# GpSimd in place of VectorE for the fifteen elimination steps of each recurrent chain

## The chip, the core and the metric

The kernel runs on one core of one Trainium2 chip. The metric is the device time of one execution in microseconds; the time before is the median of 3 runs. A profile is one execution taken by the hardware profiler. Its engines are PE (TensorE; PEld is its weight load), DVE (VectorE), ACT (ScalarE), POOL (GpSimd) and SP (SyncE, which here only issues DMAs). Each engine works through its own instructions in the order in which they were built, and an instruction waits on semaphores for what it needs from the others.

## The reference, cut to what matters

A decoder trunk of two layers over 512 tokens of width 1024. Each layer is a half-step SwiGLU feed-forward, a token mixing, and another feed-forward. The mixing runs three kinds of heads side by side on one projection: sliding-window attention, RWKV-7 time mixing (4 heads of 64) and a short convolution.

```python
for l in range(DEPTH):
    h = h + 0.5 * (1.0 + gt1) * swiglu(hn, w_ffn1_in[l], w_ffn1_out[l])
    proj = hn @ w_mix_in[l]
    y_att = sliding_window_sink_attention(p_att, ...)
    y_rwkv = rwkv7_time_mix(p_rwkv, ...)
    y_conv = short_conv_mix(p_conv, conv_w[l])
    h = h + (1.0 + gt2) * (jnp.concatenate([y_att, y_rwkv, y_conv], axis=-1) @ w_mix_out[l])
    h = h + 0.5 * (1.0 + gt3) * swiglu(hn, w_ffn2_in[l], w_ffn2_out[l])

def step(S, inp):        # in rwkv7_time_mix, scanned over the tokens
    s_kk = jnp.einsum('bhvk,bhk->bhv', S, kk_t)
    S = S * w_t[:, :, None, :] - s_kk[..., None] * (kk_t * a_t)[:, :, None, :] + v_t[..., None] * k_t[:, :, None, :]
    return S, jnp.einsum('bhvk,bhk->bhv', S, r_t)
```

## The kernel before, in words

The activations lie transposed, with features on the 128 partitions and the 512 tokens along the free dimension. Weights come from DRAM in tiles of 128x1024, and each is split into a high and a low part (L101 on ACT, L102 on DVE), so that a product is three matmuls (L90 to L92, L98).

The mixing (`mix`, from L585) weaves four generators: `products` makes the projections and, later, the output products; `rwkv(0)` and `rwkv(1)` are the recurrent chains, each with two of the four heads (called chain 0 and chain 1 here); `attention` is the attention. A loop at its end takes steps of the chains and the attention and puts projection matmuls between them in proportion to their estimated work. Then the scheduler of the tile framework sets the final order of each engine's instructions from the dependencies and its own model of durations; only passages under `manual_schedule` keep their written order. So a line that goes to another engine can change the order on all of them.

A recurrent chain does not scan over 512 tokens. It works in 8 chunks of 64, and inside a chunk the recurrence is a triangular system whose inverse is needed. The way to that inverse, in program order:

- DVE prepares the decayed operands: the running decay P (L783), its reciprocal iP (L791), the reciprocal of a norm rn (L792), kk (L794), the bonus (L800, which the head sum ps_bo of PE reads), AR, be and ka (L805 to L812).
- PE multiplies them (`pairs`, L824) into ps_c, and DVE masks the result into B (L828), whose first half LT holds the strictly triangular systems; K follows in the same way.
- The 64 diagonal blocks of 16x16 (2 heads, 8 chunks, 4 blocks) are gathered one to a partition: LT is written to DRAM as dl (L836), and eight DMAs read it back as G (L846), 64 partitions of 256 columns.
- GpSimd fills V_ (the tile `inv`) with unit matrices (L848, L849).
- Fifteen steps of elimination invert the 64 blocks side by side, each with a multiply into `elim` (L853) and a subtract in `inv` (L854): 30 instructions, each of which needs the one before it. They are 15 to 64 columns wide on 64 partitions, 680 columns in the fifteen multiplies and as many in the subtracts.
- `inv` goes to DRAM as di (L856) and comes back as C (L859, eight DMAs), from which DVE makes T (L907) and its transpose TT (L908).
- Two levels of products (L916 on PE into ps_x, ps_t and ps_tt; L921, L925, L928 on DVE) raise the inverse from blocks of 16 to 64. Then follow ps_w (L935), the chunk transitions ps_gn and ps_o (L946 to L969), and six short state steps ps_s (L977, L978).

There are two such chains in each of two layers, four in all, and 120 of the elimination instructions. The DMAs of dl, G, di and C stand in SP's queue among the loads of weights (`load_w`, L267). GpSimd's queue holds, in the feed-forwards, loads of conditioning weights (L177) and accumulating loads (L395), and in the mixing only fills.

Of the kernel before, what the change touches and what calls it, by code (L numbers as in the profile page):

```python
# [12 lines left out]
ALU = mybir.AluOpType  # L13
# [44 lines left out]
def trunk_kernel(ctx, tc, ins, out, layers=L, phases=("ffn1", "mix", "ffn2")):  # L58
    nc = tc.nc
# [11 lines left out]
    tt, stt, ts = nc.vector.tensor_tensor, nc.vector.scalar_tensor_tensor, nc.vector.tensor_scalar  # L71
# [46 lines left out]
    for i in range(KD):  # L118
        t = hp_.tile([P, T], F32, name=f"h{i}")
# [15 lines left out]
    for name, v in (("eps", EPS), ("eps64", 64 * EPS), ("gneps", GN_EPS), ("nhb", -HB)):  # L135
        t = const.tile([P, 1], F32, name=f"v_{name}")
# [71 lines left out]
    def square(i, sl):  # L208
        sq = E("sq")[:, sl]
        act(sq, h[i][:, sl], AF.Square)  # L210
        return sq
# [373 lines left out]
    def mix(l, hn, ss, mp, then, ready):  # L585
# [14 lines left out]
        def EQ(q, name):  # L600
            return mp.tile([P, T], F32, name=name, tag=f"e{q}", bufs=2)
# [154 lines left out]
        def rwkv(q):  # L756
# [38 lines left out]
            t = EQ(q, "k2")  # L795
# [42 lines left out]
            NT = 2 * NM * 2 * NB  # L838
            square = lambda t: t[:NT, : BASE * BASE].rearrange("p (t u) -> p t u", u=BASE)
            G = square(EQ(q, "G"))  # L840
            for c in range(2):
                for m in range(NM):
                    n = (c * NM + m) * 2 * NB
# [3 lines left out]
            V_ = square(EQ(q, "inv"))  # L847
            nc.gpsimd.memset(V_, 0.0)  # L848
            nc.gpsimd.memset(V_.rearrange("p t u -> p (t u)")[:, :: BASE + 1], 1.0)  # L849
            for s in range(BASE - 1):  # L850
                n = BASE - 1 - s
                t = mp.tile([NT, BASE * BASE // 4], F32, name="elim", tag=f"el{q}")[:, : n * (s + 1)].rearrange("p (t u) -> p t u", u=s + 1)
                tt(t, G[:, s, s + 1 :].unsqueeze(2).to_broadcast([NT, n, s + 1]), V_[:, s : s + 1, : s + 1].to_broadcast([NT, n, s + 1]), ALU.mult)  # L853
                tt(V_[:, s + 1 :, : s + 1], V_[:, s + 1 :, : s + 1], t, ALU.subtract)  # L854
            di = dram.tile([2 * NM, 2 * NB, BASE, BASE], F32, name="di", tag=f"di{q}", bufs=2)
            nc.sync.dma_start(di.rearrange("m n t u -> (m n) t u"), V_)  # L856
            C_ = EQ(q, "C")[:, : 2 * NB * BASE].rearrange("p (n u) -> p n u", u=BASE)
# [223 lines left out]

        prod = products()
        live, waiting = {}, {"rwkv0": lambda: rwkv(0), "rwkv1": lambda: rwkv(1), "att": attention}
        left, fill, credit = 2 * RWKV_WORK + ATT_WORK, FILL_WORK, 0.0
        more = True
# [286 lines left out]
```

## Time and profile before

| what | value |
|---|---|
| median of 3 runs | 1912.6 us (1911.94 to 1915.08) |
| profiled execution, its own time | 1913.21 us |
| its span, first to last instruction | 1911.2 us |
| granted TensorE clock, mean | 0.996 |
| mixing of the first layer | about 400 to 620 us of the span |
| mixing of the second layer | about 1340 to 1560 us of the span |
| DMA, mean | 161 GB/s |

A row of a group reads: line, engine, operation, tile written <- tiles read, shapes, count; then busy us, mean ns of one; then the idle time of the engine ahead of them and what ended it. A row of a timeline begins with the start in us from the span's start and the duration in us; a bracket gives the idle time before it and what ended that. The view by stretches gives the busy us of each engine in a stretch of the span. Tiles have the kernel's names; in rows of the built order a number behind a name tells copies of a tile apart.

### The profile page before, as it was taken

The numbers are of one execution on the slowest core, as the hardware profiler recorded it, in microseconds if no ns is written. First come the engines' busy times: TensorE is split into PE (matmuls) and PEld (weight loads), VectorE is DVE, ScalarE is ACT, GpSimd is POOL, SyncE is SP. The second block draws the span as 40 slices with busy tenths as digits, with TensorE's granted clock in tenths as the row PEclk, the third lists the DMA queues.
The fourth block names the chain that finished last, engine by engine and source line by source line (L and its number), as shares of the span: only waits on it lengthen the run. The fifth ranks groups of instructions, "written<-read, shape, count | busy, mean of one in ns | idle before, by whom it ended". The sixth has DMA issues, their size and how long they took to land. (4 is left out here: it accounts for less than half of the span.)

```text
span 1911.2 us, 37042 instructions
## 1 busy us (share of the span) xinstructions
PE 1878.8 (98%) x15504; PEld 1741.7 (91%) x15504; DVE 1399.8 (73%) x2181; ACT 837.0 (44%) x1264; POOL 130.7 (7%) x212
## 2 busy tenths in 40 slices
PE   8999999999999999999999999999999999999999
PEld 7998899897888999899899989989878899988998
DVE  7687687758976877677877776876599667864862
ACT  4443255346322554155345514544562235532551
POOL 0101100100000001110100020010000000110000
PEclk8999999999999999999999999999999999999999
DMA  7767877521312476887727678781321315774741
GB/s 300 245 168 221 271 198 229 168 70 45 79 43 81 123 198 176 278 218 199 264 62 193 171 260 242 191 278 42 93 61 49 88 34 163 209 217 130 198 140 59
DMA packets 104326, 308.46 MB, mean 161 GB/s; under 512 B 23392, under 2 KB 24416, under 8 KB 103136
## 3 DMA queue, kind: packets, MB, share of 16 engines
q1 hardware_dynamic: 75936, 203.33, 32.9%
q0 software_dynamic: 28224, 102.77, 21.7%
q8 instruction: 121, 1.98, 0.4%
q14 instruction: 45, 0.37, 0.1%
HBM read 302.66 MB, written 3.41 MB: 160 GB/s over the span
## 5 line engine op out<-in xcount | busy, mean ns | idle before, releaser
L101 ACT CAST wH<-wraw 128x1024 fp32r<-128x1024 f32 (+2 forms) x292 | 268.4, 922 | 512.6 <-PE ps_mm L91 176.8
L102 DVE TENSOR_TENSOR wL<-wraw,wH 128x1024 fp32r<-128x1024 f32 (+2 forms) x292 | 308.1, 1058 | 96.9 <-ACT wH L101 95.8
L90 PE MATMUL ps_mm<-actH,wH 128*128 128x512 f32 (+1 forms) x784 | 288.5, 368 | 0.0
L91 PE MATMUL ps_mm<-actL,wH 128*128 128x512 f32 (+1 forms) x784 | 288.0, 367 | 0.0
L92 PE MATMUL ps_mm<-actH,wL 128*128 128x512 f32 (+1 forms) x784 | 288.0, 367 | 0.0
L441 PE MATMUL ps_d<-comH,wH 128*128 128x256 f32 x816 | 226.8, 278 | 1.6 <-ACT wH L101 0.8
L443 PE MATMUL ps_d<-comH,wL 128*128 128x256 f32 x816 | 225.8, 277 | 2.3 <-DVE wL L102 2.3
L442 PE MATMUL ps_d<-comL,wH 128*128 128x256 f32 x816 | 225.5, 276 | 0.0
L98 PE MATMUL ps_mm<-hnH,wH 128*128 128x256 f32 x1040 | 214.0, 286 | 5.1 <-ACT hnH L101 2.9
L98 PE MATMUL ps_mm<-hnL,wH 128*128 128x256 f32 x1040 | 211.8, 283 | 0.0
L98 PE MATMUL ps_mm<-hnH,wL 128*128 128x256 f32 x1040 | 209.5, 281 | 0.5 <-DVE wL L102 0.5
L163 DVE SCALAR_TENSOR_TENSOR wada<-wada,crep 128x1024 f32<-128x1024 f32 x140 | 168.0, 1220 | 47.8 <-DMA wada<-in_wadaT 47.6
L102 DVE TENSOR_TENSOR wL<-sum,wH 128x1024 fp32r<-128x1024 f32 x102 | 124.8, 1224 | 74.9 <-ACT wH L101 74.7
L98 PEld LDWEIGHTS ps_mm<-hnH,wH 128*128 128x128 f32 x1040 | 159.5, 190 | 16.1 <-issue 8.2
L92 PEld LDWEIGHTS ps_mm<-actH,wL 128*128 128x128 f32 x784 | 147.8, 189 | 24.4
L90 PEld LDWEIGHTS ps_mm<-actH,wH 128*128 128x128 f32 x784 | 147.8, 189 | 24.2
L91 PEld LDWEIGHTS ps_mm<-actL,wH 128*128 128x128 f32 x784 | 147.8, 189 | 24.1
L101 ACT CAST wH<-sum 128x1024 fp32r<-128x1024 f32 x102 | 107.5, 1054 | 140.3 <-PE ps_d L442 60.1
L98 PEld LDWEIGHTS ps_mm<-hnL,wH 128*128 128x128 f32 x1040 | 160.2, 190 | 6.7 <-issue 5.7
L98 PEld LDWEIGHTS ps_mm<-hnH,wL 128*128 128x128 f32 x1040 | 160.1, 190 | 4.1 <-issue 2.9
L441 PEld LDWEIGHTS ps_d<-comH,wH 128*128 128x128 f32 x816 | 153.2, 188 | 3.9 <-ACT wH L101 1.4
L443 PEld LDWEIGHTS ps_d<-comH,wL 128*128 128x128 f32 x816 | 153.2, 188 | 2.9 <-DVE wL L102 2.9
(402 smaller groups left out, 4237.3 us busy)
## 6 DMA issues: line engine op xcount, KB each, us to landing
wada<-in_wadaT POOLq DMA_DIRECT2D x128, 512.0 KB, 4.9
wraw<-in_wmi SPq DMA_DIRECT2D x40, 512.0 KB
wraw<-in_w2p SPq DMA_DIRECT2D x36, 512.0 KB
wraw<-in_w1p SPq DMA_DIRECT2D x32, 512.0 KB
wraw<-in_w1o SPq DMA_DIRECT2D x32, 384.0 KB
wraw<-in_w2o SPq DMA_DIRECT2D x32, 384.0 KB
wraw<-in_w1i SPq DMA_DIRECT2D x20, 512.0 KB
wraw<-in_w1o SPq DMA_DIRECT2D x32, 320.0 KB
```

Of the source, the lines that this page charges most:

```text
L90: mm(acc, wH, xH, start=start, stop=False)
L91: mm(acc, wH, xL, start=False, stop=False)
L92: mm(acc, wL, xH, start=False, stop=stop)
L98: mm(acc[:, sl], w[a][:, k], x[b][:, sl], start=start and n == 0 and sl is HALVES[0], stop=stop and n == 2, skip_group_check=True)
L101: nc.scalar.copy(hi, src)
L102: nc.vector.tensor_sub(lo, src, hi.bitcast(F32))
L163: stt(w, w, 1.0, crep, ALU.mult, ALU.mult, accum_out=out_)
L441: mm(pt[:, i], wH, x[k][0], start=start and i + k == 0, stop=False, skip_group_check=True)
L442: mm(pt[:, i], wH, x[k][1], start=False, stop=False, skip_group_check=True)
L443: last = mm(pt[:, i], wL, x[k][0], start=False, stop=k == 3, skip_group_check=True)
```

## The change

The two instructions of each elimination step, L853 and L854, go from VectorE to GpSimd; `tt` is `nc.vector.tensor_tensor`. Nothing else is edited, and the arithmetic is the same.

```diff
             for s in range(BASE - 1):
                 n = BASE - 1 - s
                 t = mp.tile([NT, BASE * BASE // 4], F32, name="elim", tag=f"el{q}")[:, : n * (s + 1)].rearrange("p (t u) -> p t u", u=s + 1)
-                tt(t, G[:, s, s + 1 :].unsqueeze(2).to_broadcast([NT, n, s + 1]), V_[:, s : s + 1, : s + 1].to_broadcast([NT, n, s + 1]), ALU.mult)
-                tt(V_[:, s + 1 :, : s + 1], V_[:, s + 1 :, : s + 1], t, ALU.subtract)
+                nc.gpsimd.tensor_tensor(t, G[:, s, s + 1 :].unsqueeze(2).to_broadcast([NT, n, s + 1]), V_[:, s : s + 1, : s + 1].to_broadcast([NT, n, s + 1]), ALU.mult)
+                nc.gpsimd.tensor_tensor(V_[:, s + 1 :, : s + 1], V_[:, s + 1 :, : s + 1], t, ALU.subtract)
             di = dram.tile([2 * NM, 2 * NB, BASE, BASE], F32, name="di", tag=f"di{q}", bufs=2)
             nc.sync.dma_start(di.rearrange("m n t u -> (m n) t u"), V_)
```

The scheduler then orders the engines anew. Where the prediction speaks of it, this is what moved, in the first layer (the second is alike). DVE, behind the scans that make chain 1's decay P; C and T are chain 0's, iP is chain 1's, AR_5937 is chain 1's and X_5286 chain 0's. Before:

```order
L785 COPY pc_5885<-P_5876 128x8
L791 RECIPROCAL iP_5890<-P_5876 128x512
L853 TENSOR_TENSOR elim<-G,inv 64x55
L709 TENSOR_SCALAR gd<-gd 128x512
L854 TENSOR_TENSOR inv<-inv,elim 64x5x11
L788 TENSOR_SCALAR rn<-ps_kk 128x512
L853 TENSOR_TENSOR elim<-G,inv 64x48
L796 TENSOR_SCALAR k_5895<-a_5823,par 128x512
```

The same place in the changed kernel:

```order
L785 COPY pc_5885<-P_5876 128x8
L791 RECIPROCAL iP_5890<-P_5876 128x512
L635 SCALAR_TENSOR_TENSOR gd<-ps_mm,par,gd 128x511
L907 TENSOR_TENSOR T_5282<-C,con 128x512
L810 TENSOR_TENSOR AR_5937<-r_5617,P_5876 128x512
L908 STREAM_TRANSPOSE TT_5283<-T_5282 128x512
L709 TENSOR_SCALAR gd<-gd 128x512
L788 TENSOR_SCALAR rn<-ps_kk 128x512
```

The steps are gone from DVE, and T with its transpose moved up to stand behind chain 1's reciprocal. PE, the first products of chain 0's inverse (ps_x, then ps_t and ps_tt) before, among chain 1's products for K:

```order
L824 MATMUL ps_c<-AR_5937,iP_5890 64x128 x11
L916 MATMUL ps_x<-T_5282,B_5115 64x64 x16
L824 MATMUL ps_c<-AR_5937,iP_5890 64x128 x5
L98 MATMUL ps_mm<-hnL,wH 128x256
L98 MATMUL ps_mm<-hnH,wL 128x256 x2
```

In the changed kernel they stand behind chain 1's head sum ps_kk:

```order
L611 MATMUL ps_kk<-kksq,con 128x512
L916 MATMUL ps_x<-T_5282,B_5115 64x64 x16
L98 MATMUL ps_mm<-hnH,wH 128x256 x2
L98 MATMUL ps_mm<-hnL,wH 128x256 x2
L98 MATMUL ps_mm<-hnH,wL 128x256 x2
```

They moved ahead of chain 1's ps_bo and of its products with AR. SP, behind the load of gw, as the difference:

```order
 L998 DMA gw<-in_gw 128x256
-L267 DMA wraw<-in_wmi 128x1024
-L267 DMA wraw<-in_wmo 128x768
-L856 DMA di<-inv 64x256
-L859 DMA C<-di 16x8x16 x8
+L856 DMA di<-inv 64x256
+L859 DMA C<-di 16x8x16 x8
+L267 DMA wraw<-in_wmi 128x1024
```

Chain 0's writing of di and reading of C moved ahead of two loads of weights. On POOL the steps stand behind the fills of `inv`, with one instruction of another kind (ISA) ahead of the first of them in the program.

## The prediction

> **What bounds the kernel now.** I read the page first: its span, and the line of busy times.
>
> ```profile
> span 1911.2 us, 37042 instructions
> ...
> PE 1878.8 (98%) x15504; PEld 1741.7 (91%) x15504; DVE 1399.8 (73%) x2181; ACT 837.0 (44%) x1264; POOL 130.7 (7%) x212
> ```
>
> PE is busy for all but 32.4 us of the span. The profiled execution took 1913.21 us, 2.0 us more than its span and 0.6 us more than the median of 1912.6; I work out differences and add them to the median. VectorE (DVE) has room over the whole run, so what counts is how much PE waits in the stage that changes. The table by stretches of 40 us (PE, PEld, DVE, ACT, POOL busy, then the clock) gives that for the mixing; the last line is the sum over eight such stretches, 440 to 600 us of the first layer and 1380 to 1540 us of the second.
>
> ```profile
> 480.00:520.00 40.00, 38.86 (x354) 32.84 (x354) 36.81 (x93) 17.42 (x40) 0.43 (x2) 1.00 0.30 77
> ...
> sum 320.00, PE 307.45 PEld 263.33 DVE 256.81 ACT 124.87 POOL 1.70; mean PE 38.43 PEld 32.92 DVE 32.10 ACT 15.61 POOL 0.21
> ```
>
> In both stages together PE idles 320.0 - 307.45 = 12.6 us. DVE is at 92% there (36.81 of 40) and POOL has nothing to do: the idea of the change has a basis. But no more than 12.6 us can be won, and who makes PE wait is shown by PE's waits, here the four of 520 to 560 us, the longest of 560 to 600 us, and its like of the second layer (total, times, longest):
>
> ```profile
> PE ps_o L964 <- DVE N L954: 0.6, 1, 0.6
> PE ps_c L824 <- DVE B L828: 0.5, 1, 0.5
> PE ps_x L916 <- DVE T L907: 0.4, 1, 0.4
> PE ps_bo L611 <- DVE bonus L800: 0.4, 1, 0.4
> ...
> PE ps_s L977 <- ACT y L972: 1.4, 1, 1.4
> ...
> PE ps_s L977 <- ACT y L972: 2.2, 1, 2.2
> ```
>
> Each is one wait of 0.4 to 2.2 us. The chain steps are hidden today because the scheduler fills PE with projection matmuls meanwhile.
>
> **What leaves VectorE.** The moved steps in one layer, from the groups of 380 to 620 us:
>
> ```profile
> L854 DVE TENSOR_TENSOR inv<-inv,elim 64x15 f32<-64x15 f32 (+7 forms) x30 | 5.8, 193 | 0.6
> L853 DVE TENSOR_TENSOR elim<-G,inv 64x15 f32<-64x15 f32 (+7 forms) x30 | 5.6, 187 | 0.5
> ```
>
> 60 instructions and 11.4 us of DVE per layer (two chains of 30), 22.8 us in all. Almost none of it lies on the path: PE's waits above name the steps' neighbours (T, bonus, B, N) for 0.4 to 0.6 us each. I count 1 us per layer, 2 us in all, as won.
>
> **The latency that replaces it.** The chain is serial: dl is written to DRAM, G read back, 30 dependent steps, di written, C read back, then T on DVE and ps_x on PE. The DMA queue's rows (start and length of the issues) for chain 0 (first two), a weight load, and chain 1 (the last four):
>
> ```profile
> 479.21 0.61 SPq L836 DMA_DIRECT2D dl<-B  x1
> ...
> 482.18 2.87 SPq L846 DMA_DIRECT2D G<-dl  x8
> ...
> 509.12 0.33 SPq L267 DMA_DIRECT2D wraw<-in_wmi  x1
> ...
> 522.88 0.55 SPq L836 DMA_DIRECT2D dl<-B  x1
> ...
> 526.27 3.61 SPq L846 DMA_DIRECT2D G<-dl  x8
> ...
> 541.02 0.46 SPq L856 DMA_DIRECT2D di<-inv  x1
> 543.93 3.62 SPq L859 DMA_DIRECT2D C<-di  x8
> ```
>
> and DVE's rows at the ends of chain 1's steps, and at T:
>
> ```profile
> 532.70 0.16 DVE L853 TENSOR_TENSOR elim<-G,inv 64x15 f32<-64x15 f32 x1
> ...
> 540.79 0.17 DVE L854 TENSOR_TENSOR inv<-inv,elim 64x15 f32<-64x15 f32 x1
> ...
> 549.11 0.69 DVE L907 TENSOR_TENSOR T<-C,con 128x512 f32<-128x512 f32 x1 [0.65 <-DMA C<-di]
> ```
>
> T waits for C here, so the last landing comes 549.11 - (543.93 + 3.62) = 1.56 us after the last issue, and from the end of the steps (540.79 + 0.17) to T it is 8.15 us. By the same 1.56 us, chain 0's G is there at 482.18 + 2.87 + 1.56 = 486.6 us. GpSimd can then run without sharing its queue, whereas DVE threaded chain 0's steps through its other work.
>
> **The scheduler has already spent this.** The built order shows it. DVE, chain 0 of the first layer, behind chain 1's reciprocal (iP is its inverse decay; T, TT and X belong to chain 0's inverse); first before, then now:
>
> ```order
> L791 RECIPROCAL iP_5890<-P_5876 128x512
> L853 TENSOR_TENSOR elim<-G,inv 64x55
> L709 TENSOR_SCALAR gd<-gd 128x512
> L854 TENSOR_TENSOR inv<-inv,elim 64x5x11
> L788 TENSOR_SCALAR rn<-ps_kk 128x512
> L853 TENSOR_TENSOR elim<-G,inv 64x48
> ```
>
> ```order
> L791 RECIPROCAL iP_5890<-P_5876 128x512
> L635 SCALAR_TENSOR_TENSOR gd<-ps_mm,par,gd 128x511
> L907 TENSOR_TENSOR T_5282<-C,con 128x512
> L810 TENSOR_TENSOR AR_5937<-r_5617,P_5876 128x512
> L908 STREAM_TRANSPOSE TT_5283<-T_5282 128x512
> L709 TENSOR_SCALAR gd<-gd 128x512
> ```
>
> T stands two instructions behind the reciprocal, where before all the rest of chain 1's preparation stood between them. PE, the same place, now (before, 103 projection matmuls of L98 followed ps_kk, then ps_bo):
>
> ```order
> L611 MATMUL ps_kk<-kksq,con 128x512
> L916 MATMUL ps_x<-T_5282,B_5115 64x64 x16
> L98 MATMUL ps_mm<-hnH,wH 128x256 x2
> L98 MATMUL ps_mm<-hnL,wH 128x256 x2
> L98 MATMUL ps_mm<-hnH,wL 128x256 x2
> ```
>
> PE takes ps_x directly behind ps_kk, so a late T stops PE, with the projections queued behind it. On SP the order of chain 0's DMAs changed with it:
>
> ```order
> -L267 DMA wraw<-in_wmi 128x1024
> -L267 DMA wraw<-in_wmo 128x768
> -L856 DMA di<-inv 64x256
> -L859 DMA C<-di 16x8x16 x8
> +L856 DMA di<-inv 64x256
> +L859 DMA C<-di 16x8x16 x8
> +L267 DMA wraw<-in_wmi 128x1024
> ```
>
> The first weight load that is now behind the wait for the steps was issued at 509.12 us. The C reads are all issued 547.55 - 540.96 = 6.6 us after the steps end, so the load keeps its time if they end by 502.5 us; beyond that it is late by as much, and a load that is late by more than PE's own wait would starve the projections.
>
> When does PE get to ps_x? DVE's rows of before, then PE's:
>
> ```profile
> 499.23 0.19 DVE L853 TENSOR_TENSOR elim<-G,inv 64x63 f32<-64x63 f32 x1
> 499.35 0.27 DVE L783 TENSOR_TENSOR_SCAN P<-decay,zero 128x64 f32<-128x64 f32 x1
> ...
> 500.93 0.73 DVE L635 SCALAR_TENSOR_TENSOR gd<-ps_mm,par,gd 128x511 f32<-128x511 f32 x1
> ...
> 502.11 3.35 DVE L791 RECIPROCAL iP<-P 128x512 f32<-128x512 f32 x1
> ```
>
> ```profile
> 503.88 1.02 PE L611 MATMUL ps_kk<-kksq,con 128*128 128x512 f32 x2
> ...
> 517.03 1.13 PE L611 MATMUL ps_bo<-bonus,con 128*128 128x512 f32 x2 [0.37 <-DVE bonus L800]
> ```
>
> PE is through ps_kk at 504.9 us. DVE ended iP at 505.46; the 12 steps ahead of it from 496 us on are gone, at 0.12 us a slot (499.23 to 499.35), so it ends near 504.0, and gd (0.73 us) takes it to 504.7 us. T needs about 0.6 us before ps_x. So C must be there by 504.3 us, and the 30 steps may last 504.3 - 486.6 - 8.15 = 9.5 us, 0.32 us a step. After that the new order holds: I followed DVE's and PE's rows to ps_bo and found both there within 0.3 us of each other.
>
> Chain 1: in the new order PE has 158 L98 matmuls between the products for B and ps_x; at (517.03 - 0.37 - 504.9) / 103 = 0.114 us that is 18.0 us. The small matmuls among them, from the groups of 526 to 549.8 us:
>
> ```profile
> L977 PE MATMUL ps_s<-St,GT 64*64 64x64 f32 x24 | 2.0, 242 | 0.0
> L893 PE MATMUL ps_xv<-vN,K 64*64 64x64 f32 x32 | 1.4, 221 | 0.0
> ...
> L983 PE MATMUL ps_ys<-RT,St 64*64 64x64 f32 x28 | 1.0, 218 | 0.0
> ```
>
> These are 4.4 us; with two head sums of 1 us (as ps_kk above), the transposes and the products for K I estimate 9 us, 27 us together. About 1.5 us of it, two pieces of 0.7 us on DVE, pass until B is in SBUF. From B's end (522.88 us, dl's issue) to G's landing (526.27 + 3.61 + 1.56 = 531.4) it takes 8.5 us, then come the steps, then 8.15 us. That leaves 27 - 1.5 - 8.5 - 8.15 = some 9 us: the two chains have about the same allowance, 9.5 and 9.
>
> **What a step costs on GpSimd.** No arithmetic on GpSimd is in the trace. The nearest rows are its fills:
>
> ```profile
> 468.92 0.30 POOL L848 MEMSET inv<- 64x256 f32 x1 [76.88 <-DVE es L1043]
> 469.28 0.12 POOL L849 MEMSET inv<- 64x16 f32 x1
> ...
> 391.05 0.99 POOL L1015 MEMSET Sc<- 128x512 f32 x2 [34.00 <-DVE wL L102]
> ```
>
> A fill of 16 columns takes 0.12 us, of 256 columns 0.30 us: 0.108 us fixed and 0.77 ns a column, and 0.06 us to the next dependent one. Lower end: 30 steps at 0.12 + 0.06 are 5.4 us, on time. Upper end: the 512-column fill, 0.5 us, and the gap, 0.56 us: 16.8 us, late by some 7.5 us. [...] 0.216 + 0.104 + 0.06 = 0.38 us, near the 0.36 us from the 256-column fill to the next one. I take 0.40 us, 12.0 us for the 30 steps. Late: 12.0 - 9.5 = 2.5 us and 12.0 - 9 = 3 us, 5.5 us per layer, 11 us in both. Less the 2 us won: +9 us, **1921.6 us**.
>
> [...]
>
> **The code of the new operation.** POOL's order has one new kind of row, ahead of the first step:
>
> ```order
> L848 MEMSET inv 64x256
> L849 MEMSET inv 64x16
> L853 ISA
> L853 TENSOR_TENSOR elim<-G,inv 64x15
> L854 TENSOR_TENSOR inv<-inv,elim 64x15
> ```
>
> It follows the fill of 469.28 us, 17 us ahead of G's landing, so whatever it loads is hidden unless it takes over 17 us. I price it at 0; without that cover it would add its own length to chain 0 of the first layer alone. [...]
>
> **Rivals.**
>
> *On time (0.30).* Steps of up to 0.32 us end within the allowance. For it: the scheduler placed T and ps_x at just this point, and its other placements hold within 0.4 us (PE's wait for T above). Against it: the 0.36 us between two plain fills. PE then waits about as before: 1911 to 1915 us.
>
> *Taking turns, or a slow GpSimd (0.20).* Steps are held up by DVE. DVE's work between 486.6 and 498 us that reads two SBUF tiles:
>
> ```profile
> L1050 DVE TENSOR_TENSOR Sc<-Sc,den 128x512 f32<-128x512 f32 x2 | 1.4, 692 | 0.0
> ...
> L102 DVE TENSOR_TENSOR wL<-wraw,wH 128x1024 fp32r<-128x1024 f32 x1 | 1.2, 1205 | 0.0
> ...
> L1048 DVE TENSOR_TENSOR den<-den,es 128x4 f32<-128x4 f32 x2 | 0.3, 158 | 0.0
> ```
>
> With three more groups like the last, 3.8 us: if steps wait for all of it, 15.8 us a chain; with steps of 0.56 us, 16.8 us. Late by 6.3 to 7.8 us a chain, four times, less 2 us: +24 to +28, 1937 to 1941 us, and more if both hold. Nothing in the trace of before shows such turns: the fills of 256 columns kept their 0.30 us with DVE busy, by their group:
>
> ```profile
> L848 POOL MEMSET inv<- 64x256 f32 x4 | 1.2, 304 | 246.7 <-DVE es L1043 153.8 <-DVE k L798 92.9
> ```
>
> [...]
>
> *Faster (0.08).* Steps well within 0.3 us, and the room on DVE removes waits of PE. One place pays: PE's wait of 1.4 us for y (2.2 us in the second layer), which comes where DVE and ACT serve chain 1's tail; with the four waits of 0.4 to 0.6 us in both layers, 1.4 + 2.2 + 2 x 1.9 = 7.4 us at most, 1905 us; two thirds of it make 1908 us. It decides if chain 1 comes over 2 us earlier in relation to PE. Against it: the rows of the tail stand in the order they had.
>
> That the steps do not move can be left out: POOL's order has them.
>
> **How the numbers follow.** My forecast, late steps with 1917 to 1935 us, has 0.42. A measurement of this kernel can tell about 0.2%, 3.8 us, from no change, so it and the rival of turns are slower (0.62), on time is the same (0.30), the last is faster (0.08). The range leaves out the faster rival below 1909 us and the worst of turns and slow steps together, above 1945 us.
>
> **What would show it.** Right: steps on POOL 0.36 to 0.45 us apart; PE waiting for T (L907) at both ps_x of L916 for 2 to 3 us each, the wait before T on DVE being for C; L853 and L854 gone from DVE, with no other PE wait grown by over 1 us. Wrong: steps under 0.32 us and no wait for T (on time), steps stretched just where DVE runs L102 or L1050 (turns), a gap between the ISA row and the first step that lasts beyond 486.6 us (code), or weight loads on SP that land late behind C.

## The result and the profile after

| | before | after |
|---|---|---|
| median | 1913.84 us (1911.94 to 1917.14, 4 runs) | 1925.46 us (1923.9 to 1930.98, 4 runs) |
| profiled execution, its span | 1913.21, 1911.2 us | 1924.62, 1922.9 us |

The changed kernel is slower: ratio 1.0064, 95% interval 1.0039 to 1.009, 11.6 us between the medians and 11.7 us between the spans. Where it lies is shown by the view by stretches, cut at the first `ps_ks` and the last `ps_g` of each mixing stage (length, then busy us of PE, PEld, DVE, ACT, POOL, then clock). Before:

```profile
399.34:606.18 206.84, 200.35 (x2307) 172.72 (x2308) 152.10 (x322) 87.50 (x184) 0.85 (x4) 1.00 0.26 73
1335.74:1544.50 208.76, 201.67 (x2306) 173.88 (x2307) 152.09 (x322) 87.56 (x184) 0.85 (x4) 0.99 0.25 72
sum 415.60, PE 402.02 PEld 346.60 DVE 304.19 ACT 175.06 POOL 1.70; mean PE 201.01 PEld 173.30 DVE 152.10 ACT 87.53 POOL 0.85
```

and after:

```profile
400.30:612.23 211.93, 201.76 (x2306) 174.22 (x2307) 143.18 (x262) 88.04 (x184) 20.06 (x64) 0.99 0.25 71
1341.12:1556.38 215.26, 202.25 (x2306) 174.81 (x2307) 143.02 (x262) 88.06 (x184) 20.48 (x64) 0.98 0.24 70
sum 427.19, PE 404.01 PEld 349.03 DVE 286.20 ACT 176.10 POOL 40.54; mean PE 202.00 PEld 174.52 DVE 143.10 ACT 88.05 POOL 20.27
```

The stages are 427.19 - 415.60 = 11.6 us longer, which is all of it. PE's waits in them grew from 13.6 to 23.2 us (+9.6) and PE's busy time by 2.0 us, at a lower clock. VectorE is busy 18.0 us less; the steps' rows add up to 22.8 us, but rows of VectorE overlap (the step of 499.23 us lasts 0.19 us and the next instruction starts at 499.35). PE's waits for T in the second layer's stage before (the first layer's line, 0.4 us, stands in the prediction):

```profile
PE ps_x L916 <- DVE T L907: 0.6, 2, 0.4
```

After, PE's waits of the first layer's stage, then of the second's:

```profile
PE ps_x L916 <- DVE T L907: 5.2, 2, 2.9
PE ps_s L977 <- ACT y L972: 1.6, 2, 1.1
...
PE ps_bo L611 <- DVE bonus L800: 0.6, 1, 0.6
```

```profile
PE ps_x L916 <- DVE T L907: 6.8, 2, 3.9
PE ps_s L977 <- ACT y L972: 2.9, 2, 2.4
```

Waits for T are 12.0 us instead of 1.0. Those for N and B are gone and one of two for bonus is left; with what grew a little elsewhere, all other waits together are 1.4 us less. GpSimd's first steps of chain 0 and the last ones of chain 1 in the first layer, then T on VectorE for the two chains:

```profile
487.69 0.20 POOL L853 TENSOR_TENSOR elim<-G,inv 64x15 f32<-64x15 f32 x1 [17.27 <-DMA G<-dl]
487.97 0.22 POOL L854 TENSOR_TENSOR inv<-inv,elim 64x15 f32<-64x15 f32 x1
...
551.34 0.21 POOL L854 TENSOR_TENSOR inv<-inv,elim 64x15 f32<-64x15 f32 x1
```

```profile
507.54 0.69 DVE L907 TENSOR_TENSOR T<-C,con 128x512 f32<-128x512 f32 x1 [2.62 <-DMA C<-di]
...
559.70 0.69 DVE L907 TENSOR_TENSOR T<-C,con 128x512 f32<-128x512 f32 x1 [6.26 <-DMA C<-di]
```

The first step waits for G, not for code. From first step to last end the four chains took 12.07, 11.68, 12.38 and 11.79 us. They are not 30 even steps. In the middle of chain 0, GpSimd:

```profile
492.09 0.30 POOL L854 TENSOR_TENSOR inv<-inv,elim 64x63 f32<-64x63 f32 x1
492.48 1.23 POOL L853 TENSOR_TENSOR elim<-G,inv 64x64 f32<-64x64 f32 x1
493.78 0.31 POOL L854 TENSOR_TENSOR inv<-inv,elim 64x64 f32<-64x64 f32 x1
494.18 0.68 POOL L853 TENSOR_TENSOR elim<-G,inv 64x63 f32<-64x63 f32 x1
```

and VectorE at the same time:

```profile
492.34 1.21 DVE L102 TENSOR_TENSOR wL<-wraw,wH 128x1024 fp32r<-128x1024 f32 x1
...
494.00 0.69 DVE L1050 TENSOR_TENSOR Sc<-Sc,den 128x512 f32<-128x512 f32 x1
```

A step that meets one of these ends 0.16 or 0.17 us behind it (493.71 and 493.55; 494.86 and 494.69); the steps beside these two start 0.36 to 0.40 us apart. In chain 1 of this layer the stretched steps (0.62, 0.80 and 0.88 us) stand beside L993, L994 and L102, which read two SBUF tiles as well.

### The profile page after: what moved, and what is told of

The parts are those of the page before. It is cut to its first block, busy times and chain, and to the rows that moved or that the text cites. A ratio compares the mean times of both kernels' runs of the same rounds, so it can differ in the third digit from the quotient of the medians.

```text
span 1922.9 us, 37068 instructions
## 1 busy us (share of the span) xinstructions
PE 1881.7 (98%) x15504; PEld 1744.9 (91%) x15504; DVE 1381.7 (72%) x2061; ACT 838.5 (44%) x1264; POOL 170.0 (9%) x332
## 5 line engine op out<-in xcount | busy, mean ns | idle before, releaser
L102 DVE TENSOR_TENSOR wL<-wraw,wH 128x1024 fp32r<-128x1024 f32 (+2 forms) x292 | 308.5, 1060 | 110.5 <-ACT wH L101 109.4
L102 DVE TENSOR_TENSOR wL<-sum,wH 128x1024 fp32r<-128x1024 f32 x102 | 124.9, 1225 | 73.8 <-ACT wH L101 73.6
```

Source lines behind the costliest of these rows:

```text
L102: nc.vector.tensor_sub(lo, src, hi.bitcast(F32))
```

## The experiments

The theory: the loss is T, late for the place that the order gives to ps_x. Rivals: GpSimd is too slow wherever ps_x stands; taking turns with VectorE is the whole loss; the two chains hinder each other; and behind the waits, the clock.

**One chain at a time: e1_chain0 and e2_chain1** (q == 0, then q == 1; the cut is against the kernel before, and "..." stands for arguments that stay)

```
+ el = nc.gpsimd.tensor_tensor if q == 0 else tt
- tt(t, G...)      - tt(V_...)
+ el(t, G...)      + el(V_...)
```

> The steps of chain 0 run on GpSimd, those of chain 1 on VectorE as before. Theory (late T): the loss sits in PE's waits for T, each chain for itself. Chain 0's waits stay at 2.3 us (first layer) and 3.9 us (second), chain 1's go to under 0.7 us; against the kernel before that is +6.2 us less about 1 us of relief on VectorE, near +5 us, ratio 1.0027. Rival (interplay): the loss comes from both chains being on GpSimd, so one alone costs nothing, ratio 1.000. Rival (relief is worthless or negative): all of the 12 us are in one chain, so this one shows +0 or +12 us.

> The steps of chain 1 run on GpSimd, those of chain 0 on VectorE as before. Theory (late T): chain 1's waits for T stay near 2.9 us in each layer, chain 0's near those of before (0.4 us); +5.8 us less about 1 us, near +5 us, ratio 1.0025. Rival (interplay): ratio 1.000. Both theories are silent on what the scheduler does with a chain 1 that is now faster in its reckoning than chain 0: if it puts ps_x earlier, the wait grows by as much.

Measured: 1913.23 us, ratio 1.0002 (0.9992 to 1.0011), and 1926.58 us, ratio 1.0071 (1.0056 to 1.0087). Neither is the +5 us of the theory. The medians are 0.6 and 14.0 us above the kernel before, and by them alone the rival that puts the whole loss into one chain would fit. The traces speak against it, for in the changed kernel PE waits for both chains' T. In e1_chain0 the waits for T are 2.3 and 1.0 us in the first layer, 2.3 and 0.8 in the second, 6.4 in all, and its profiled stages last 419.3 us, 3.7 more than before. That execution took 1915.74 us, the second longest of ten, with two stretches of lower clock (lowest 0.78 and 0.50 over 5 us). A part of what pays for the waits is PE's busy time: 199.13 us in its second stage, which has no such stretch, against 200.35 in the first stage before; the rest isn't explained. In e2_chain1 chain 1 is late by 6.0 and 5.0 us, not by 2.9, so one chain alone can lose it all and the rival of interplay falls. Its steps and PE's wait:

```profile
531.32 0.20 POOL L853 TENSOR_TENSOR elim<-G,inv 64x15 f32<-64x15 f32 x1 [15.91 <-DMA G<-dl]
...
541.27 0.21 POOL L854 TENSOR_TENSOR inv<-inv,elim 64x15 f32<-64x15 f32 x1
```

```profile
549.55 0.58 PE L916 MATMUL ps_x<-T,B 64*64 64x64 f32 x5 [6.05 <-DVE T L907]
```

The steps take 10.16 us here, less than in the changed kernel (11.7), for VectorE ran nothing with two SBUF inputs meanwhile. But PE is at ps_x at 549.55 - 6.05 = 543.5 us, 12.2 us after the first step; in the changed kernel it was 557.5, 17.7 us after. So neither the engine alone nor the length of the steps sets the wait: the place in the order does, and the scheduler moved it.

**T later in the order: e3_later1, e4_later_both, e5_both_fit.** In each, `got['T1'] = tt(T4, ...)` keeps the instruction and a later one on VectorE is made to come first:

```
  e3  + bi = ts(cv, u, ...)                          # L721
      + q and behind(got['T1'], bi)
  e4  + bi = ts(t, a_, ...)                          # L796
      + q and behind(got['T0'], bi)
      + the same for T1 behind the last tap of the convolution (L723)
  e5  T0 as in e4, T1 as in e3
```

> The changed kernel with one more dependence: chain 1's T on VectorE comes behind the first of the convolution's products of its half (L721), which puts PE's ps_x of chain 1 26 projection matmuls, 26 x 0.114 = 3.0 us, later in the order; the steps stay on GpSimd, as long as they were. Theory (late T): PE's two waits of 2.9 us for chain 1's T go to under 0.5 us each, chain 0's stay at 2.3 and 3.9 us; 5.3 us off the changed kernel, near 1920 us (ratio to the kernel before 1.0035), and 1 to 2 us more if the clock dips behind those waits cost anything. Rival (taking turns, or GpSimd too slow wherever it is placed): the wait turns up again at the next place that needs T (ps_w2 or ps_gn), 1925 us, ratio 1.0064.

> The changed kernel with two more dependences: chain 0's T comes behind chain 1's k2 factor on VectorE (L796), 24 projection matmuls or 2.7 us later, and chain 1's T behind the last tap of the convolution (L723), so that it stays behind C in spite of what moved ahead of it. Theory (late T): no wait for T over 1.3 us is left (the second layer's chain 0, 3.9 - 2.7 = 1.2 us); 10 to 12 us off the changed kernel, 1913.5 to 1915.5 us, ratio 0.999 to 1.001 to the kernel before; down to 1911 us (0.9985) if the clock dips behind the waits cost the 2.9 us by which PE's busy time had grown. Rival (turns, or GpSimd too slow wherever it is placed): the waits move to ps_w2, ps_gn or ps_s, 1922 to 1926 us.

> Both chains on GpSimd; chain 0's T behind L796 as in e4_later_both, where PE did not wait for it in either layer, and chain 1's T behind L721 as in e3_later1, where PE did not wait for that one. Theory (late T): no wait for T over 1 us, PE waits some 12 us less than in the changed kernel, the two mixing stages last about 414 us (before 415.6, after 427.2 us), 1911 to 1913 us, ratio 0.999 to 1.000. Rival (what a later T saves comes back in the tail): PE's wait for y at the first ps_s of chain 1 grows to 3 to 4 us in both layers, as it did in the first layer of e3_later1 (3.4 us); 1914 to 1916 us, ratio 1.001 to 1.002.

Measured: e3_later1 1919.84 us, ratio 1.0039 (1.0026 to 1.0052), the time that was expected, but not by the waits as expected (in the profiled stages PE waits 21.9 us instead of 23.2): chain 1's waits are gone in both layers; chain 0's are 4.0 and 4.3 us, since the reads of C were issued 3.7 and 4.0 us after di instead of 2.1 and 3.5. In the first layer, 3.4 us of wait for y stood in the tail instead of 1.1, so part came back, as the rival had it. e4_later_both: 1919.06 us, 1.0031 (1.0017 to 1.0045), e5_both_fit: 1920.03 us, 1.0034 (1.0022 to 1.0046); both missed. Chain 0's waits are gone in both, but chain 1's stand at 4.2 and 2.1 us in e4 and 4.6 and 3.5 us in e5, though C was there. In e5, SP's rows, ACT's, then VectorE's:

```profile
548.20 0.46 SPq L856 DMA_DIRECT2D di<-inv  x1
550.32 4.58 SPq L859 DMA_DIRECT2D C<-di  x8
555.01 0.84 SPq L267 DMA_DIRECT2D wraw<-in_wmo  x2
```

```profile
558.25 0.83 ACT L101 CAST wH<-wraw 128x768 fp32r<-128x768 f32 x1 [8.67 <-DMA wraw<-in_wmo]
```

```profile
559.11 0.96 DVE L102 TENSOR_TENSOR wL<-wraw,wH 128x768 fp32r<-128x768 f32 x1 [4.36 <-ACT wH L101]
...
560.98 0.69 DVE L907 TENSOR_TENSOR T<-C,con 128x512 f32<-128x512 f32 x1
```

By the prediction's 1.56 us behind the last issue (554.90) C is there at about 556.5 us, and T comes at 560.98. What it waited for is a weight load that stands on SP behind di's wait for the steps.

**That load apart: e9_load_apart**

```
  def load_w(..., dge=nc.sync):   # new argument: the queue that issues the load
- w = load_w(wo1[l, i, :, :6], 6)
+ w = load_w(wo1[l, i, :, :6], 6, dge=nc.scalar if i == 2 else nc.sync)
```

> e5_both_fit with one edit: the third load of the output projection's weights is issued from ScalarE's queue instead of SP's, so that it no longer stands behind the wait of di for chain 1's steps. The orders of PE and VectorE are the same, row for row. In e5_both_fit that load was issued at 555.0 us, behind the reads of C; ScalarE waited 8.7 us for it, VectorE split it at 559.1 us, and T, queued behind that on VectorE, came 4.6 us late for PE although C had been there since about 556.5 us. Theory (late weight load on SP): the split moves to about 554 us, T is held by C alone until 556.5 to 557 us, PE's waits for chain 1's T go from 4.6 and 3.5 us to under 1 us; 7 us and the clock dips behind those waits less than 1920 us, 1911 to 1913 us, ratio 0.999 to 1.000. Rival (the steps on GpSimd are too slow for chain 1 in any order): T still 3 us late or more, 1918 to 1920 us, ratio 1.003.

Measured: 1910.61 us, ratio 0.9989 (0.9979 to 0.9999), as expected; the rival falls. The load is issued at 545.45 us, and T and PE are:

```profile
554.16 0.95 DVE L102 TENSOR_TENSOR wL<-wraw,wH 128x768 fp32r<-128x768 f32 x1
...
556.03 0.68 DVE L907 TENSOR_TENSOR T<-C,con 128x512 f32<-128x512 f32 x1
```

```profile
556.27 0.39 PE L98 MATMUL ps_mm<-hnL,wH 128*128 128x256 f32 x2
556.77 0.92 PE L916 MATMUL ps_x<-T,B 64*64 64x64 f32 x24
```

PE comes from the projections to ps_x without a wait; in the second layer it waits 0.5 us. This profile is of the fastest of twelve executions (1907.45 us). All 60 steps of a layer are on GpSimd and the loss is gone: the engine was not too slow, the order was wrong for it. The kernel before with the same load moved was not run, so this doesn't show that GpSimd is better than VectorE here.

**Fewer steps: e7_few** (`for s in range(10)` in place of `range(BASE - 1)`)

> The changed kernel with the last 10 of the 30 steps of each chain left out (the inversion stays incomplete, so the output is not the reference's). By the order that results, the scheduler then puts ps_x earlier by 9 to 17 projection matmuls, 1.0 to 1.9 us, which is 0.1 to 0.19 us a step, while a step takes 0.40 us in the trace with what holds it up. Theory (late T, because the scheduler takes a GpSimd step for a VectorE one): the chain ends 4 us earlier and is wanted 1 to 2 us earlier, so every wait for T shrinks by 2 to 3 us, from 2.3 to 3.9 us to 0 to 1.5 us; 1914 to 1917 us, ratio 1.001 to 1.002. Rival (the wait has nothing to do with the steps' length, but with the two transfers and DVE's queue): waits as in the changed kernel, 1924 us.

Measured: 1914.73 us, ratio 1.0002 (0.9991 to 1.0012). The 20 steps take 8.23 to 8.44 us a chain, and the waits for T are 1.0 us in the first layer and 0.4 and 2.1 in the second (the last a little over what was expected), 3.4 in all instead of 12.0. The rival falls. Ten steps less moved chain 1's ps_x by 17 matmuls of 0.114 us, the upper end of the 9 to 17: by this the scheduler reckons with 0.19 us a step or less, at most about VectorE's time, where GpSimd takes 0.34 to 0.40.

**A step by itself: e8_probe.** Only the steps are run, in eight sections; for each, GpSimd starts with the 64x15 multiplication and ends with the 64x15 subtraction.

> No part of the reference is computed: the 30 steps alone, on constant data, in eight sections one behind the other. GpSimd does them with VectorE idle; with VectorE multiplying two SBUF tiles of 128x512; one of PSUM with one of SBUF; one SBUF tile by a constant; with reciprocals of one SBUF tile; multiplying two SBUF tiles of 128x1024; idle again; and last VectorE does the steps. Theory (a step costs 0.345 us by itself and is held up by VectorE's instructions with two SBUF inputs alone): 10.3 us for 30 steps in the sections with VectorE idle, with PSUM, with one input and with reciprocals; one step per VectorE instruction or worse beside two SBUF inputs, so 20 us and more until VectorE is through. Rival (VectorE in any form slows GpSimd, or none does and the stretched steps in the kernel have another cause): all sections with VectorE busy alike. On VectorE the steps should take 30 x 0.20 = 6 us, and if the code load ahead of the first step matters, the first idle section is longer than the second.

Rows of GpSimd with VectorE idle (first and last step), beside 128x512 of two SBUF inputs (first two steps), and beside one SBUF input (last step). Then VectorE's own first and last step, and its groups with two SBUF inputs and with PSUM:

```profile
8.80 0.21 POOL L82 TENSOR_TENSOR el_none<-G_none,inv_none 64x15 f32<-64x15 f32 x1 [0.28 <-DVE x_none L109]
...
18.74 0.21 POOL L86 TENSOR_TENSOR inv_none<-inv_none,el_none 64x15 f32<-64x15 f32 x1
...
19.87 0.71 POOL L82 TENSOR_TENSOR el_two<-G_two,inv_two 64x15 f32<-64x15 f32 x1 [0.27 <-DVE x_two L109]
20.67 0.66 POOL L86 TENSOR_TENSOR inv_two<-inv_two,el_two 64x15 f32<-64x15 f32 x1
...
67.51 0.39 POOL L86 TENSOR_TENSOR inv_one<-inv_one,el_one 64x15 f32<-64x15 f32 x1
```

```profile
117.58 0.17 DVE L82 TENSOR_TENSOR el_dve<-G_dve,inv_dve 64x15 f32<-64x15 f32 x1
...
124.35 0.17 DVE L86 TENSOR_TENSOR inv_dve<-inv_dve,el_dve 64x15 f32<-64x15 f32 x1
```

```profile
L92 DVE TENSOR_TENSOR x_two<-a,b 128x512 f32<-128x512 f32 x20 | 13.8, 692 | 0.7
L93 DVE TENSOR_TENSOR x_psum<-p,b 128x512 f32<-128x512 f32 x20 | 13.8, 691 | 0.7
```

| VectorE beside the steps | 30 steps |
|---|---|
| idle, first and second time | 10.15, 10.14 us |
| PSUM and SBUF 128x512; reciprocals | 10.15; 10.15 us |
| one SBUF input 128x512 by a constant (0.43 us each) | 13.84 us |
| two SBUF inputs 128x512 (0.69 us each) | 17.86 us; 0.73 us a step while they last |
| two SBUF inputs 128x1024 (1.23 us each) | 20.5 us |
| (steps on VectorE, GpSimd idle) | 6.94 us |

The theory was right on two inputs, PSUM and reciprocals, wrong on one input by a constant, which held GpSimd up too (13.84 us against 10.15). Beside two SBUF inputs of 128x512 GpSimd did one step (0.73 us) per VectorE instruction, while VectorE kept its 0.69 us, as beside PSUM. The first section was not longer than the second (10.15 and 10.14 us): no code load shows.

**Chain 0 alone, and placed: e6_chain0_fit** (e1_chain0 with T0 behind L796)

> Chain 0 on GpSimd with its T behind L796, chain 1 on VectorE. In e1_chain0 PE waited 2.3 us for chain 0's T in each layer and 1.0 and 0.8 us for chain 1's. Theory (late T): the two waits of 2.3 us go and with them the clock dip behind one of them; the mixing stages, 419.3 us in e1_chain0, last 412 to 414 us; 1908 to 1911 us, ratio 0.998 to 0.999, faster than the kernel before by about what VectorE was relieved of. Rival (no relief to be had): as the kernel before, 1912.6 us, ratio 1.000.

Measured: 1907.27 us, ratio 0.9966 (0.9954 to 0.9978), faster than both kernels, 0.7 us below what the theory had. The stages:

```profile
398.85:603.95 205.10, 198.86 (x2306) 172.07 (x2307) 148.50 (x292) 87.85 (x184) 10.63 (x34) 1.00 0.26 73
1332.15:1538.48 206.33, 199.13 (x2306) 172.26 (x2307) 148.58 (x292) 87.88 (x184) 10.96 (x34) 1.00 0.26 73
sum 411.43, PE 397.99 PEld 344.33 DVE 297.08 ACT 175.73 POOL 21.59; mean PE 199.00 PEld 172.17 DVE 148.54 ACT 87.86 POOL 10.80
```

The stages are 4.2 us shorter than before, 4.0 of it in PE's busy time; PE waits 13.4 us, as before (13.6). The two profiled spans differ by 5.8 us; the rest lies outside the stages, where nothing was changed. About 1.6 us of the 4.0 is a clock dip that this run has not and the kernel before has (0.68 for 5 us). The other 2.4 us stay open. e9_load_apart has a lower busy time too (398.39 us in both stages, 402.02 before). e7_few, with its steps on GpSimd and T where the scheduler puts it, has 200.14 us in its first stage, without a dip, near the 200.35 of before. So GpSimd alone doesn't bring it; whether the order would without GpSimd, no run shows.

## Why the prediction was right, and where not

- **The mechanism.** The forecast was 1921.6 us by T late at both ps_x; measured 1925.46, inside the range, with 0.62 on slower. By its own sum: T late by 11 us, measured 11.0 more than before (12.0 - 1.0); won 2 us, measured 1.4 us of waits; together +9.6 instead of +9. The parts are less close than the sum: 2.3, 2.9, 3.9 and 2.9 us late, where 2.5, 3, 2.5 and 3 were forecast, so that the two 11s meet is in part luck.
- **The missing term.** The other 2.0 us are PE's busy time: after two of the four waits for T PE ran at a lower clock for some us (0.66 from 560 to 565 us, 0.50 from 1450 to 1455 us). By the stretches of 5 us that is an estimated 4 us, against 1.6 us for the one dip before (0.68). That these waits cost more than their length was not in the sum.
- **The step's price.** 12.0 us a chain against 11.7 to 12.4. The 0.40 us was right as a mean and wrong in its makeup: a step costs 0.34 us by itself (e8_probe 10.15 us, e2_chain1 10.16; from start to start 0.29 us at 15 columns, 0.37 to 0.39 at 64; the 30 steps are 10.15 / 6.94 = 1.46 times VectorE's), and taking turns adds 1.5 to 2.2 us a chain. No run shows the 0.216 and the 0.104 us in the sum for a step, which were the author's estimates; the probe's rows with VectorE idle last 0.21 us at 15 columns and 0.29 to 0.31 at 64, with 0.07 to 0.08 us to the next. The turns that the sum left out filled the difference: that the mean came out is luck. Turns were a rival, priced at 3.8 us more for chain 0; they are half of that, and hold together with the forecast. Without turns, four chains of 10.15 us would be late by some 7 us less in all; that was worked out, not run. So the loss has two parts: the length of the chain, where turns make some 7 of the 11 us by which T is late, and the place of ps_x; e9_load_apart shows that the place, with the load that it holds up, can undo all of it.
- **Turns with VectorE.** That the rival of turns counted VectorE's work on two SBUF tiles alone was the author's assumption; the trace of before did not show it. The probe bears it out for two SBUF inputs of 128x512: beside them a GpSimd step lasts until VectorE's instruction is through (about 0.66 us instead of 0.21 to 0.31), beside PSUM it doesn't (0.21 to 0.31 us). It does not bear out the "alone": beside one SBUF input by a constant the steps took 13.84 us instead of 10.15. On VectorE's side nothing shows, for it kept its 0.69 us.
- **The allowance.** G was predicted for 486.6 us, 487.6 in the time of the run after, whose stage began 0.96 us later; the first step came at 487.69. PE was at ps_x at 508.38 - 2.26 = 506.1 (predicted 504.9 + 0.96 = 505.9) and at 557.5. From the last step to T it took 7.8, 8.2, 8.8 and 7.6 us (8.15), and from T to ps_x 0.7 to 0.8 us (0.6). The second layer's 8.8 is a read of C issued 3.45 us after di instead of 2.1; PE waited 3.9 us there.
- **The code of the new operation, SP's weight load.** Both free, as predicted: the first step waited for G (487.69 us), the probe's two idle sections took 10.15 and 10.14 us, and in the first layer ScalarE waited 4.0 us for loads of the input weights, 4.2 before. But the hazard that was named, a load held up behind C, is what undid e4 and e5: it was looked for at one load only, where chain 1's di stood in front of another.
- **What would show it.** Of the signs for right, T waited for C and no other wait of PE grew by over 1 us, but the steps were not 0.36 to 0.45 us apart: most were 0.28 to 0.40, three in each chain 0.66 to 1.35. One of the signs for wrong came too, steps stretched beside L102 and L1050 (and L993, L994). It didn't rule out the forecast, since both can hold at once.

## What to carry to other kernels

Moving a serial chain to an idle engine changes when its result comes, and a list scheduler that reckons the new engine as fast as the old one will place the consumer too early (here at 0.19 us a step or less, where GpSimd took 0.34 to 0.40); look in the built order where the first consumer stands, and hold it back there if the chain is longer than reckoned. Look at every queue in which the chain's last transfer waits, for whatever stands behind it is late too (here a weight load, issued behind C at 555.0 us in e5_both_fit and at 545.45 us in e9_load_apart). For a chain on GpSimd, look at what VectorE runs beside it: here its instructions with two SBUF inputs added 1.5 to 2.2 us to 10.15.

## What was not expected of the hardware

After some of its waits PE ran at a lower granted clock. In the changed kernel, around the wait of 3.9 us that ends at 1450.8 us (the fields as above):

```profile
1440.00:1445.00 5.00, 4.78 (x33) 3.27 (x33) 4.96 (x7) 2.22 (x3) 0.88 (x4) 1.00 0.07 16
1445.00:1450.00 5.00, 1.92 (x12) 1.09 (x10) 0.76 (x3) 1.91 (x2) 0.00 (x0) 0.89 0.14 13
1450.00:1455.00 5.00, 4.18 (x42) 4.10 (x43) 4.97 (x8) 0.63 (x1) 0.00 (x0) 0.50 0.00 0
1455.00:1460.00 5.00, 5.00 (x111) 4.71 (x110) 3.20 (x3) 0.00 (x0) 0.00 (x0) 0.92 0.38 108
```

Over the mixing stages of ten traces, all eight waits of 3.5 us and more were followed by such a dip (lowest stretch of 5 us 0.50 to 0.73), 9 of 17 waits of 1.7 to 3.4 us, and none under 1.7 us. What decides among these 17 no run shows: in the changed kernel the wait of 2.91 us for T that ends at 560.44 us has a stretch at 0.66 behind it, and the one of 2.88 us that ends at 1504.64 us has none below 1.00.
